# Differential attention: the second map's factor in a stage of its own, and another order of the last head's token tiles

## The chip, the cores and the metric

The kernel runs on one core of one Trainium2 chip. The metric is the time of one execution on the device, in microseconds (us), the median of several runs. A core has engines that run side by side and wait for each other by semaphores: PE (TensorE, matrix products and transposes), DVE (VectorE), ACT (ScalarE), POOL (GpSimd) and SP, which issues the transfers. Each engine works through its own queue strictly in order: an instruction that waits holds everything behind it on its engine.

## The reference, cut to what matters

The reference is a chain of two model blocks. The change lies in one part, the differential attention of the second block's second layer (`diff_attention`), 8 heads, 528 tokens (16 meta tokens and 512 others):

```python
def attn_map(qb, kk):
    lg = jnp.einsum('bqhd,bshd->bhqs', qb, kk).astype(jnp.float32) * scale + bias
    return jax.nn.softmax(jnp.where(mask, lg, NEG_INF), axis=-1)

a = attn_map(q1b, k1) - lam * attn_map(q2b, k2)
return jnp.einsum('bhqs,bshd->bqhd', a.astype(vb.dtype), vb)
...
o = rms_norm(o, sub_g) * (1.0 - lam_init)
return o.reshape(B, Tp, N_HEADS * B_V_DIM) @ w_o
```

So each head has two softmax maps; the second, times `lam`, is subtracted from the first, and the difference is applied to the values. Since each head's output is normalized afterwards, a common factor of a row may be left in it until then.

## The kernel before, in words

`layer_b` computes this layer. A unit is one head `h` and one tile `b` of 128 query tokens, `b` from 1 to 4; unit `b` sees `L` = 16 + 128 b keys (144, 272, 400 or 528), so `b` = 4 is the longest. The 32 units go through a software pipeline, `pipeline`: in round i, each letter of `STAGES_B` runs one stage on the unit that entered `lag` rounds ago, in the order of the letters.

- `l` and `m` (lag 0): the logits of the first and the second map on PE (tile `lg`).
- `s` and `r` (lag 0): `soft` for either map. DVE adds the bias and finds the row's extreme (L1633, and L1637 where two halves are needed), ACT takes the exponential and, as it goes, the row sum (tile `p`, L257). The first map's sum goes to a column of `sn` (`G["e"]`), the second's to a column of `sxb` (`s`).
- `d` (`s_diff`, lag 2): the factor of the second map, -lam times the first sum over the second, by a reciprocal on DVE (L1908) and two small ACT instructions on `sxb`; then `p` = `p2` times factor plus `p` on DVE, a scalar_tensor_tensor. I call this last one the combine.
- `t` (`turn`, lag 4): PE transposes `p` into `tp`, ACT copies it to `pt`.
- `o` (`s_out`, lag 6): PE multiplies with the values (`po`), DVE copies the result into `o`, ACT squares it.

After a head's last unit, `ends` puts three steps into `late`, one per round: the scaling of `o` (DVE and ACT on `sn`), the transposes `ot` with ACT's `ah`, and DVE's `al`. Only then can the head's share of the output projection run.

Between the stages `more` hands out filler for PE, by the credits of `FILL_B`: first the projections that make the later heads' queries, keys and values (tiles `hq` and `tg`; DVE scales them by `rb` into `hd`, ACT squares `hd` into `hsq`, PE sums `hsq` into `hs`, from which ACT makes the norm `hf`), and, when these are used up, the first part of the output projection (`wo`). The small products of the meta tokens (`ml`, `mo`) are handed out likewise. Weights come by transfer into `ws`, and ACT and POOL split them into a high part `wh` and a low part `wl`; POOL also makes the low parts `kx` and `qx` of keys and queries. Tiles in PSUM (`hq`, `tg`, `lg`, `tp`, `po`, `hs`, `wo` and the like) share eight banks in turn, so a product may wait until an earlier tile in its bank has been read.

The order of all instructions is as written, so PE's queue is set when the program is built.

Of the kernel before, what the change touches and what calls it, by code (L numbers as in the profile page):

```python
# [48 lines left out]
SQ_A, SQ_B = 0, 0  # L49
LN_EXP = "natural_log_exp_and_others"  # L50
TOP_V, TOP_D, TOP_R, TOP_E = (1, 1, 1, 1, 2), 275, 270, 60
STAGES_A, STAGES_B = "ldmtosw", "tlsdmro"
FILL_A, FILL_B = {"t": 1, "l": 1, "o": 2, "w": 2}, {"t": 0.868, "l": 1.017, "m": 1.562, "o": 1.471, "r": 0.7, "d": 0.1, "s": 0.1}
META_A, OUT_A, EARLY_B = 9, 2, 3
SUMS, ENDS = 3, 7
# [2 lines left out]
ORDER_B = (2, 3, 1, 4)  # L58
# [171 lines left out]
class K:  # L230
# [9 lines left out]
    def t(self, dt=F32, name="t", n=TB):  # L240
        x = self.pool.tile([128, TB], dt, name=name, tag="t")
        return x[:, :n] if n != TB else x
# [13 lines left out]
    def act(self, out, x, f=AF.Identity, **k):  # L256
        self.nc.scalar.activation(out, x, f, **k)  # L257
# [4 lines left out]
    def stt(self, out, in0, scalar, in1, op0, op1, **k):  # L262
        self.nc.vector.scalar_tensor_tensor(out, in0, scalar, in1, op0=op0, op1=op1, **k)  # L263
# [1050 lines left out]
    def head_sums(self, sq, ones, dim):  # L1314

        f = self.t(F32, "hf")
        for c in self.HALVES:
            S_ = self.sm("hs")[:, 0:264]
            for y in sq:
                self.mm(S_, ones[y.dtype], y[:, c], y is sq[0], y is sq[-1])  # L1320
            self.act(f[:, c], S_, AF.Ln, bias=self.eps[1e-6], scale=1.0 / dim)
        self.act(f, f, AF.Exp, scale=-0.5)
# [97 lines left out]
    def layer_a(self, hs, norm, hg):  # L1420
# [175 lines left out]
        def end(i):  # L1596
            if i == len(U) + OUT_A:
                self.out_late("w_oa", ao, out, 2, range(KD))

        a, b, c = LAG_A  # L1600
        S_ = {"m": (s_mask, 0), "t": (self.turn, 2 + b), "d": (s_share, 2 + a), "l": (s_logits, 2),
              "o": (s_out, 2 + c), "s": (s_soft, 2), "w": (s_low, 2 + c)}
        self.pipeline(U, S_, STAGES_A, more, lambda i: i >= META_A and meta and meta.pop(0)(), end)
        assert not meta and not topk
# [135 lines left out]
    def layer_b(self, hs, norm, hx):  # L1740

        nc, A, v, t, stt, dve, act = self.nc, self.A, self.v, self.t, self.stt, self.dve, self.act
# [49 lines left out]
        def place(h):  # L1792
            if ao[h] is None:
                ao[h] = t(F32R, "ah"), t(F32R, "al")
            return ao[h]
# [16 lines left out]
        def turn_o(o, n, w=4):  # L1812
            tp = self.sm("ot")
            for j in range(w):
                nc.tensor.transpose(tp[:, n * j:n * j + n], o[:n, 128 * j:128 * j + 128], self.ident[:n, :n])
            return tp[:, :w * n]

        def low(lo, ps, hi):
            stt(lo, ps, sub, hi.bitcast(F32), MUL, SUB)

        def ends(G):

            def turn():
                G["tp"] = turn_o(G["o"], 128)
                act(place(G["h"])[0][:, META:T], G["tp"], scale=sub)

            def last():
                hi, lo = (x[:, META:T] for x in ao[G["h"]])
                low(lo, G["tp"], hi)
                ready[1].add(G["h"])  # L1830

            return [lambda: scale(G["o"], G["e"], 128), turn, last]
# [43 lines left out]
            next(steps)  # L1876
        U = []
        for h in range(8):
            G = {"h": h}
            U += [{"b": b, "h": h, "G": G} for b in ORDER_B]  # L1880

        def s_logits(u, i):
            h = u["h"]
            q0, L = self.queries(u["b"])
            while ("q", h) not in done:
                next(steps, None)
            u["ps", i] = self.pair_logits(i, done["q", h], slice(q0, q0 + 128), done["k", h], L)

        def s_soft(u, i):
            h, b, G = u["h"], u["b"], u["G"]  # L1890
            L = self.queries(b)[1]
            if "e" not in G:
                G["e"] = stat()
                for k in ([0, 1] if h == 0 else [h + 1] if h < 7 else []):
                    self.bias[k] = self.load_bias(self.bias_d[k])
                if h:
                    self.bias[h - 1] = None
            if i == 0:
                u["s"] = self.small.tile([128, 8], F32, name="sxb", tag="sxb", bufs=8)
            s = u["s"]  # L1900
            x = u["p", i] = t(F32, "p", L)
            self.soft(x, u.pop(("ps", i)), self.bias[h][:, T - L:], s[:, 2 * i:2 * i + 2], s[:, 6 + i:7 + i],
                      s[:, 4:5] if i else G["e"][:, 3 + b:4 + b])

        def s_diff(u):

            s, b = u["s"], u["b"]
            nc.vector.reciprocal(s[:, 4:5], s[:, 4:5])  # L1908
            act(s[:, 4:5], s[:, 4:5], scale=nlam)
            act(s[:, 5:6], s[:, 4:5], scale=u["G"]["e"][:, 3 + b:4 + b])  # L1910
            u["p"], p2 = u.pop(("p", 0)), u.pop(("p", 1))
            stt(u["p"], p2, s[:, 5:6], u["p"], MUL, ADD)

        def s_out(u):
            G, b = u["G"], u["b"]
            if "o" not in G:
                G["o"] = t(F32, "o", 512)
            while ("v", u["h"] // 2) not in done:
                next(steps)
            o = self.pv(u, vh, tokens=True)  # L1920
            nc.vector.tensor_copy(G["o"][:, 128 * b - 128:128 * b], o)
            junk = self.b2.tile([128, 128], mybir.dt.bfloat16, name="oj", tag="oj", bufs=2)
            act(junk, o, AF.Square, accum_out=G["e"][:, b - 1:b])
            if b == ORDER_B[-1]:
                late.extend(ends(G))

        restored = []
# [58 lines left out]
            return late or others  # L1986

        a, b, c = LAG_B
        S_ = {"t": (self.turn, b), "d": (s_diff, a), "o": (s_out, c)}
        for i in range(2):  # L1990
            S_["lm"[i]] = (lambda u, i=i: s_logits(u, i)), 0
            S_["sr"[i]] = (lambda u, i=i: s_soft(u, i)), 0
# [58 lines left out]
```

## Time and profile before

| what | us |
|---|---|
| median of 3 runs | 2362.16 |
| lowest and highest of them | 2360.67, 2363.61 |
| the profiled execution | 2363.21 |
| its span in the trace | 2361.4 |
| the pipelined rounds of this attention in the trace, about | 1712 to 1960 |

The span is what the trace covers, from the first to the last instruction; the profiled execution's own time has 1.8 us more around it, and is itself 1.05 us above the median of the runs. A time in the trace is counted from the span's start. "Busy" is time in which an engine works on an instruction. "PEclk" is the TensorE clock that was granted, as a share of full speed.

### The profile page before, as it was taken

What the parts mean: (1) busy time and instruction counts of PE and PEld (TensorE: products, weight loads), DVE (VectorE), ACT (ScalarE), POOL (GpSimd) and SP (SyncE); (2) the same over time, 40 slices, a digit from 0 to 9 for tenths busy, and PEclk for the clock granted to TensorE, in tenths of its full rate; (3) what the DMA queues carried; (4) which work ended last, traced back from release to release, by engine and by line L of the source; (5) the groups of instructions that cost most, each with busy time, mean ns of one, the idle gap of its engine ahead of it and who ended that gap; (6) DMA issues with size and microseconds to landing.
All of it is one profiled execution on the core that took longest, in us unless ns stands there. A gap on an engine that the chain in (4) does not pass through costs nothing.

```text
span 2361.4 us, 36818 instructions
## 1 busy us (share of the span) xinstructions
PE 2286.5 (97%) x14560; PEld 2052.0 (87%) x14560; DVE 1296.8 (55%) x2492; ACT 982.4 (42%) x1814; POOL 1066.4 (45%) x608
## 2 busy tenths in 40 slices
PE   7999999999999999998999999999999989999999
PEld 5777787878888888888889999999998888989898
DVE  7767995566573022129974734435456656625443
ACT  3445543352243133344454423324466654424332
POOL 0434534456434434665533443434764443444433
PEclk9999999999999999999999999999999999999999
DMA  8324434525443223342102332323322122332322
GB/s 281 108 90 130 145 104 138 171 85 169 129 161 107 90 89 91 91 135 91 55 10 85 93 110 72 108 72 90 95 73 73 50 64 63 90 107 81 109 79 90
DMA packets 95980, 240.68 MB, mean 102 GB/s; under 512 B 10560, under 2 KB 26048, under 8 KB 95808
## 3 DMA queue, kind: packets, MB, share of 16 engines
q1 hardware_dynamic: 95808, 238.32, 33.0%
q8 instruction: 115, 1.88, 0.3%
q14 instruction: 57, 0.47, 0.1%
HBM read 230.72 MB, written 4.33 MB: 100 GB/s over the span
## 4 chain that ended last, share of the span: by engine, by line
PE 73%; DVE 14%; ACT 7%; issue 3%; DMA 2%; POOL 1%; SPq 0%; ACTq 0%; DVEq 0%; POOLq 0%
PE mm L260 54%; PE dn L260 9%; PE hq L260 2%; DVE cv L263 2%; PE tg L260 2%; ACT wh L210 1%; DVE xbc L263 1%; PE po L260 1%; ACT p L257 1%; PE lg L260 1%; DVE score L1476 1%; DMA ada<-in_w_ada_dram 1%; DVE p L263 1%; DVE pw L245 1%; DVE hd L245 1%
## 5 line engine op out<-in xcount | busy, mean ns | idle before, releaser
L266 POOL TENSOR_TENSOR wl<-ws,wh 128x1024 fp32r<-128x1024 f32 (+3 forms) x353 | 836.3, 2374 | 1084.8 <-ACT wh L210 1002.2
L260 PE MATMUL mm<-hh,wh 128*128 128x264 f32 (+3 forms) x2280 | 610.9, 322 | 10.5 <-ACT hh L257 7.6
L260 PE MATMUL mm<-hh,wl 128*128 128x264 f32 (+3 forms) x2280 | 605.6, 320 | 1.5 <-POOL wl L266 1.5
L260 PE MATMUL mm<-hl,wh 128*128 128x264 f32 (+3 forms) x2280 | 605.7, 320 | 1.4 <-DVE hl L263 0.7
L210 ACT CAST wh<-ws 128x1024 fp32r<-128x1024 f32 (+3 forms) x361 | 365.2, 1020 | 218.7 <-PE dn L260 83.7
L260 PEld LDWEIGHTS mm<-hh,wh 128*128 128x128 f32 x2280 | 381.7, 190 | 47.8 <-ACT hh L257 9.6
L260 PEld LDWEIGHTS mm<-hl,wh 128*128 128x128 f32 x2280 | 380.5, 189 | 38.9 <-DVE hl L263 5.3
L260 PEld LDWEIGHTS mm<-hh,wl 128*128 128x128 f32 x2280 | 381.3, 190 | 33.1 <-POOL wl L266 2.3
L263 DVE SCALAR_TENSOR_TENSOR cv<-u,vecs,cv 128x527 f32<-128x527 f32 (+3 forms) x176 | 185.9, 1056 | 87.6 <-ACT cv L257 84.5
L260 PE MATMUL dn<-ch,wl 128*128 128x264 f32 (+1 forms) x528 | 140.7, 321 | 0.0
L260 PE MATMUL dn<-ch,wh 128*128 128x264 f32 (+1 forms) x528 | 140.7, 321 | 0.0
L260 PE MATMUL dn<-cl,wh 128*128 128x264 f32 (+1 forms) x528 | 140.6, 320 | 0.0
L245 DVE TENSOR_TENSOR u<-mm,rb 128x264 f32<-128x264 f32 (+1 forms) x176 | 67.3, 424 | 108.2 <-PE mm L260 107.4
L257 ACT ACTIVATE cv<-u,vecs 128x528 f32<-128x528 f32 (+1 forms) x88 | 72.5, 824 | 115.2 <-DVE u L245 114.9
L260 PE MATMUL hq<-hh,wh 128*128 128x264 f32 x384 | 116.6, 304 | 1.6 <-ACT pt L1668 0.9
L260 PE MATMUL hq<-hh,wl 128*128 128x264 f32 x384 | 109.8, 286 | 2.7 <-POOL wl L266 2.7
L260 PE MATMUL hq<-hl,wh 128*128 128x264 f32 x384 | 110.1, 287 | 0.0
L263 DVE SCALAR_TENSOR_TENSOR junk<-ada,cs 128x512 bf16<-128x512 f32 x96 | 101.6, 1096 | 12.2 <-DMA ada<-in_w_ada_dram 12.0
L260 PE MATMUL mm<-ul,wh 128*128 128x512 f32 x256 | 100.9, 394 | 0.0
L260 PE MATMUL mm<-uh,wl 128*128 128x512 f32 x256 | 100.8, 394 | 0.0
L260 PE MATMUL mm<-uh,wh 128*128 128x512 f32 x256 | 100.7, 394 | 0.0
L260 PEld LDWEIGHTS dn<-ch,wl 128*128 128x128 f32 x528 | 87.6, 188 | 7.8 <-POOL wl L266 0.3
(368 smaller groups left out, 4177.3 us busy)
## 6 DMA issues: line engine op xcount, KB each, us to landing
ws<-in_w_up_dram SPq DMA_DIRECT2D x120, 512.0 KB, 3.6
ws<-in_w_in_dram SPq DMA_DIRECT2D x65, 512.0 KB, 3.6
ada<-in_w_ada_dram SPq DMA_DIRECT2D x96, 256.0 KB, 5.6
ws<-in_w_down_dram SPq DMA_DIRECT2D x32, 512.0 KB, 3.7
ws<-in_w_dn_dram SPq DMA_DIRECT2D x32, 512.0 KB, 3.5
E<-acs_d SPq DMA_DIRECT2D x32, 256.0 KB, 4.4
ws<-in_w_bs_dram SPq DMA_DIRECT2D x16, 512.0 KB, 3.7
ws<-in_w_ia_dram SPq DMA_DIRECT2D x15, 512.0 KB, 3.6
```

The source lines that it names most:

```text
L210: k.nc.scalar.copy(hi[:, :n_], st[:, :n_])
L245: self.nc.vector.tensor_tensor(out, in0, in1, op=op)
L257: self.nc.scalar.activation(out, x, f, **k)
L260: self.nc.tensor.matmul(out, a, b, start=start, stop=stop)
L263: self.nc.vector.scalar_tensor_tensor(out, in0, scalar, in1, op0=op0, op1=op1, **k)
L266: (eng or self.nc.vector).tensor_tensor(out, x, hi.bitcast(F32), op=SUB)
L1476: nc.vector.match_replace(s, m8, s, GONE)
```

## The change

`s_diff` is split in two. The reciprocal and the two small ACT instructions become the stage `f` (`s_factor`, lag 1), which stands behind `r` in each round; `s_diff` (lag 2) keeps only the combine. And the last head takes its tiles in the order 4, 3, 2, 1 where before it took 2, 3, 1, 4, as all other heads still do. `f` has no entry in `FILL_B`, so it hands out no filler, and no instruction is added or taken away.

```diff
-STAGES_A, STAGES_B = "ldmtosw", "tlsdmro"
+STAGES_A, STAGES_B = "ldmtosw", "tlsdmrfo"
...
-            G = {"h": h}
-            U += [{"b": b, "h": h, "G": G} for b in ORDER_B]
+            G = {"h": h, "order": ORDER_B if h < 7 else (4, 3, 2, 1)}
+            U += [{"b": b, "h": h, "G": G} for b in G["order"]]
...
-        def s_diff(u):
+        def s_factor(u):
 
             s, b = u["s"], u["b"]
             nc.vector.reciprocal(s[:, 4:5], s[:, 4:5])
             act(s[:, 4:5], s[:, 4:5], scale=nlam)
             act(s[:, 5:6], s[:, 4:5], scale=u["G"]["e"][:, 3 + b:4 + b])
+
+        def s_diff(u):
+
+            s = u["s"]
             u["p"], p2 = u.pop(("p", 0)), u.pop(("p", 1))
             stt(u["p"], p2, s[:, 5:6], u["p"], MUL, ADD)
...
-            if b == ORDER_B[-1]:
+            if b == G["order"][-1]:
                 late.extend(ends(G))
...
-        S_ = {"t": (self.turn, b), "d": (s_diff, a), "o": (s_out, c)}
+        S_ = {"t": (self.turn, b), "f": (s_factor, 1), "d": (s_diff, a), "o": (s_out, c)}
```

On DVE, in the round whose two softmaxes have `L` = 400, near 1827 us of the trace, these rows stand before:

```order
L1633 ISA p,sxb<-lg,bias 128x400
L1633 ISA sxb 128x1
L1908 RECIPROCAL sxb<-sxb 128x1
L263 SCALAR_TENSOR_TENSOR p<-p,sxb 128x528
L245 TENSOR_TENSOR hd<-hq,rb 128x264
L1633 ISA p,sxb<-lg,bias 128x400
L1633 ISA sxb 128x1
L1921 COPY o<-po 128x128
```

and these with the change:

```order
L1633 ISA p,sxb<-lg,bias 128x400
L1633 ISA sxb 128x1
L263 SCALAR_TENSOR_TENSOR p<-p,sxb 128x528
L245 TENSOR_TENSOR hd<-hq,rb 128x264
L1633 ISA p,sxb<-lg,bias 128x400
L1633 ISA sxb 128x1
L1909 RECIPROCAL sxb<-sxb 128x1
L1926 COPY o<-po 128x128
```

The combine (128x528 here) keeps its place; the reciprocal, now of the unit one round younger, stands behind the second softmax.

On ACT the same round reads so, with what goes and what comes (`kx` and `hsq` belong to a later head's projection, `p,sn` is the exponential of the first map, `p,sxb` that of the second):

```order
 L1390 CAST kx<-hd 64x528 x2
 L257 ACTIVATE p,sn<-p,sxb 128x400
-L257 ACTIVATE sxb<-sxb,lam 128x1
-L257 ACTIVATE sxb<-sxb,sn 128x1
 L257 ACTIVATE hsq<-hd 128x528
 L210 CAST wh<-ws 128x1024
 L257 ACTIVATE p,sxb<-p,sxb 128x400
+L257 ACTIVATE sxb<-sxb,lam 128x1
+L257 ACTIVATE sxb<-sxb,sn 128x1
 L257 ACTIVATE oj,sn<-po 128x128
```

The two small instructions leave the place behind the first exponential and come behind the second.

At the end of the rounds, when no unit enters any more, DVE's queue changes like this (`mo` is the meta tokens' output, `o` and `sn` belong to head 6 and its scaling):

```order
-L1908 RECIPROCAL sxb<-sxb 128x1
-L263 SCALAR_TENSOR_TENSOR p<-p,sxb 128x144
-L1921 COPY o<-po 128x128
+L263 SCALAR_TENSOR_TENSOR p<-p,sxb 128x272
+L1909 RECIPROCAL sxb<-sxb 128x1
+L1926 COPY o<-po 128x128
 L245 TENSOR_TENSOR sn<-sn 16x2
 L263 SCALAR_TENSOR_TENSOR sn<-sn 16x2
 L245 TENSOR_TENSOR mo<-mo,sn 16x256
-L1908 RECIPROCAL sxb<-sxb 128x1
-L263 SCALAR_TENSOR_TENSOR p<-p,sxb 128x528
```

The last unit's combine follows behind the last of these rows: with the change it is 128x144 instead of 128x528, and no reciprocal stands right ahead of it.

## Rows read from the trace of the kernel before

**Rows 1.** The page's first part: PE's busy time, share, instructions.

```profile
PE 2286.5 (97%) x14560; PEld 2052.0 (87%) x14560; DVE 1296.8 (55%) x2492; ACT 982.4 (42%) x1814; POOL 1066.4 (45%) x608
```

**Rows 2.** Busy time by stretch: length, each engine, granted clock, DMA.

```profile
core 0: us, PE busy (x) PEld busy (x) DVE busy (x) ACT busy (x) POOL busy (x), PEclk, DMA share, GB/s
1712.00:1945.00 233.00, 217.27 (x1700) 208.60 (x1699) 139.80 (x425) 149.32 (x455) 118.68 (x82) 0.97 0.22 65
1945.00:1960.00 15.00, 9.81 (x78) 8.98 (x76) 7.25 (x21) 7.35 (x25) 0.07 (x1) 1.00 0.04 15
1724.00:1730.00 6.00, 5.83 (x32) 5.52 (x33) 1.70 (x8) 5.05 (x10) 2.14 (x2) 0.72 0.01 3
1840.00:1846.00 6.00, 5.34 (x36) 5.30 (x37) 2.34 (x13) 5.57 (x14) 4.76 (x4) 0.72 0.48 132
1908.00:1916.00 8.00, 7.19 (x40) 6.87 (x41) 3.89 (x16) 5.16 (x16) 5.17 (x4) 0.57 0.33 94
```

**Rows 3.** What PE waited for, 1712 to 1945: us, times, longest.

```profile
PE hs L260 <- ACT hsq L257: 7.2, 6, 1.9
PE ml L260 <- POOL qk L1785: 2.6, 2, 2.2
PE po L260 <- DVE mp L245: 1.5, 1, 1.5
PE wo L260 <- POOL wl L266: 1.2, 1, 1.2
PE hq L260 <- ACT pt L1668: 0.9, 1, 0.9
PE wo L260 <- DVE sn L1843: 0.9, 1, 0.9
PE lg L260 <- DMA qx<-qz: 0.8, 1, 0.8
PE ot L1815 <- DVE o L245: 0.3, 1, 0.3
PE ot L1815 <- DVE sxb L1908: 0.3, 1, 0.3
```

**Rows 4.** What DVE waited for, the same stretch, the longest in total.

```profile
DVE p L263 <- ACT sxb L257: 51.7, 32, 3.6
```

**Rows 5.** Instructions on the tile sxb: count, ns shortest/median/longest, first, last.

```profile
L1908 DVE RECIPROCAL sxb<-sxb x32: 141/153/160, 1719.6 to 1944.0; 128x1 f32<-128x1 f32 x32
L257 ACT ACTIVATE sxb<-sxb,lam x32: 277/278/296, 1721.3 to 1944.2; 128x1 f32<-128x1 f32 x32
L257 ACT ACTIVATE sxb<-sxb,sn x32: 294/295/296, 1721.6 to 1944.5; 128x1 f32<-128x1 f32 x32
L263 DVE SCALAR_TENSOR_TENSOR p<-p,sxb x32: 367/921/3357, 1721.9 to 1944.8; 128x272 f32<-128x272 f32 x8, 128x400 f32<-128x400 f32 x8, 128x144 f32<-128x144 f32 x8, 128x528 f32<-128x528 f32 x8
```

**Rows 6.** Order of time near 1830 us: start, duration, instruction [idle before].

```profile
1827.44 2.70 POOL L266 TENSOR_TENSOR kx<-hd,kx 64x528 fp32r<-64x528 f32 x2 [0.54 <-POOL qk L1785]
...
1829.25 1.46 DVE L263 SCALAR_TENSOR_TENSOR p<-p,sxb 128x528 f32<-128x528 f32 x1 [2.05 <-ACT sxb L257]
1830.63 0.42 DVE L245 TENSOR_TENSOR hd<-hq,rb 128x264 f32<-128x264 f32 x1
...
1831.08 0.64 ACT L257 ACTIVATE hsq<-hd 128x528 f32<-128x528 f32 x1 [1.86 <-DVE hd L245]
...
1831.78 1.16 PE L260 MATMUL hs<-hsq,halves 128*128 128x264 f32 x4 [1.90 <-ACT hsq L257]
```

**Rows 7.** Order of time in the last rounds, the same columns.

```profile
1944.84 0.77 DVE L263 SCALAR_TENSOR_TENSOR p<-p,sxb 128x528 f32<-128x528 f32 x1 [0.69 <-ACT sxb L257]
1945.53 0.28 DVE L1921 COPY o<-po 128x128 f32<-128x128 f32 x1
...
1947.66 0.66 PE L1815 MATMUL ot<-ident,o 128*128 128x128 f32 x4 [2.14 <-DVE o L245]
...
1948.70 2.73 PE L260 MATMUL po<-v,pt 128*128 128x128 f32 x22
...
1953.67 0.66 PE L1815 MATMUL ot<-ident,o 128*128 128x128 f32 x4 [2.24 <-DVE o L245]
```

## The prediction

> **What bounds the kernel now.** I read the page's first part, then busy time by stretch, then the waits of PE, of DVE and of ACT in the stretch that the change touches, and last the order of time at single places. PE is busy for 97% of the span [rows 1], so only the time in which PE stands still, or runs at a lower clock, can be won. By stretch [rows 2]: from 1712 to 1945 us, the rounds of the attention, PE is busy for 217.3 of 233 us, so 15.7 us are idle; in the last rounds, 1945 to 1960, it is busy for 9.8 of 15, so 5.2 are. ACT is busy for 64% and DVE for 60% of the rounds: neither has too much work, so PE's idle time comes from order, from what stands ahead of what in a queue. The nine rows of PE's waits add up to the same 15.7 us [rows 3]. Most of it, 7.2 in six waits, is for `hsq`, the squares from which the later heads' norms are summed. A third loss is the clock: in three short stretches the granted clock is 0.72, 0.72 and 0.57 of full [rows 2], so PE falls between its two levels, 1.2 and 2.4 GHz. That costs about 6 x 0.28 = 1.7, 1.7 and 8 x 0.43 = 3.4 us, 6.8 in all. The first follows the `hs` wait that ended at 1724, the second the `ml` wait, the third the waits for `wl` and `qx`. All I can win or lose here is then 15.7 + 5.2 + 6.8 = 27.7 us, about 1.2%.
>
> **Where the idle time comes from.** DVE waits 51.7 us, 32 times, for the two small ACT instructions on `sxb` [rows 4]: 1.6 us for each unit. Before the change the combine needs a reciprocal made just ahead of it and, behind that, two small instructions of ACT, which stand behind the first map's exponential in ACT's queue. Near 1830 us this is seen whole [rows 6]: the combine starts after 2.05 us of waiting; behind it stands `hd`, at 1830.63; ACT was idle for 1.86 us for that `hd` and squares it at 1831.08; PE was idle for 1.90 us and starts `hs` at 1831.78. The same chain, a stalled combine and behind it `hd`, stands ahead of the other five `hs` waits.
>
> **What the change moves.** The reciprocal (0.15 us) and the two ACT instructions (0.28 and 0.30) run 32 times as before [rows 5], 23 us of work, none added. They come behind the second softmax of the round before, so that a combine finds its factor ready when the round's first softmax is done. No transfer and no instruction of POOL or SP changes its place, and PE's queue differs only in the last head. The terms:
>
> 1. *The `hs` waits.* They are 1.2 us on average, and the stall of the combine ahead of them is 1.6. With the stall gone `hd` comes early enough in all six, if the combine then runs. It reads two tiles from SBUF, and it is long where POOL works: near 1830 it took 1.46 us for 528 columns and ended 0.57 us after POOL's `kx` had (1827.44 + 2.70 = 1830.14), while the last one took 0.77 [rows 6, 7]. In the order of time, POOL works in three of the six places at the time to which the combine moves. I take 5.5 of 7.2; bounds 0 and 7.2.
> 2. *Other waits behind the combine on DVE:* `ml` 2.6 (its `qk` comes from an `hd` two combines later), `hq` 0.9 (a bank freed by `pt`, behind the second exponential), `wo` 0.9, `ot` 0.3 and 0.3, together 5.0 [rows 3]. I take 3.5; bounds 0 and 5.0.
> 3. *Waits that POOL sets:* `po` behind `mp` 1.5 (DVE's scaling of `o`, under POOL), `wl` 1.2, `qx` 0.8, together 3.5 [rows 3]. The combine is not their last cause. I take 0.5; bounds 0 and 3.5.
> 4. *The clock.* The stretches at 1724 and 1840 follow waits that go by terms 1 and 2; I count their 3.4 us back and leave the third. Bounds 0 and 6.8.
> 5. *The last rounds.* `ot` of head 6 waits 2.14 us for `o` [rows 7]. Its last copy, at 1945.53, stands right behind the last combine, which waited 0.69 us and took 0.77. With the change the factor is there, and the combine has 144 columns; the shortest of all took 0.37 [rows 5]. So 0.69 + 0.40 = 1.1 us. Behind this `ot` there were 5 transposes and 22 passes of `po` in 2.73 us; with tile 1 last there are 2 and 18, which saves 4 x 0.124 = 0.5 us and, at the same price, 0.4 for the transposes. The longer products of tile 4 now lie ahead of `ot`, inside its wait. The end of head 7 (2.24 us of waiting for its scaling) is as long as before. Together 2.0; bounds 0 and 2.9.
> 6. *Waits that come up instead.* When PE arrives some 9 us earlier, what POOL makes for it (term 3, of which 3.0 remain) comes into sight more often. I put this at 2.0, two thirds of it; bounds 0 and 4.
>
> Sum: -5.5 - 3.5 - 0.5 - 3.4 - 2.0 + 2.0 = -12.9 us. The profiled execution took 2363.2, so 2350.3; it was 1.05 above the median of the runs, so 2349.3 against that median.
>
> What hides the moved work: ACT's second exponential runs while DVE makes the reciprocal, and the factor then has until the next round's first softmax. If that cover is gone, because DVE reaches the reciprocal late (some filler of DVE stands ahead of it, at the place shown none), then ACT stands before the two small instructions, and behind them `oj` and `pt` are late, and so `tp`'s bank and PE's next product. The lag of two rounds from `turn` to the output covers `pt` itself, not the bank. The new order in the last head puts 528 columns into two rounds in a row and then less in each; PE showed no wait in the rounds of that head up to the `wo` wait of 0.9, so I cost this at nothing.
>
> **The rivals.**
>
> *The combine stalls at POOL instead.* POOL is busy for 118.7 of 233 us [rows 2], 51%, in instructions of 1.4 us. A combine that starts earlier meets one in half the cases and ends behind it. Then about half of terms 1 and 2 and one of the two clock stretches stay: -3.5 - 2.0 - 1.7 - 2.0 + 2.0 = -7.2, 2355. For it: combines took from 0.37 to 3.36 us with a median of 0.92 [rows 5]. Against it: the stalls under POOL are in the trace of before already, and the wait for ACT is paid on top of them; only where the wait covered POOL's time is it replaced. The Trainium skill ("SBUF — State Buffer", section on the two separate sides) says that GpSimd and a VectorE instruction with two SBUF inputs take a shared port pair as an exclusive lock, held for the whole instruction, and that the loser blocks fully. The trace agrees near 1830 (the combine ended 0.57 us after `kx`). By that rule taken alone the wait would only change its name at the places where POOL works; that is the 2355 worked out above.
>
> *It is hidden.* ACT, not DVE, may be what is late: its queue has casts of weights and keys and two exponentials in each round, and `hsq` may be held by these once `hd` is early. Then about 1 us of the `hs` waits and the 2 us of the last rounds are won: 2359. Against it: ACT was idle for 1.86 us ahead of `hsq` [rows 6], and it is free for 36% of the rounds.
>
> *It is slower.* The reciprocal stands behind the second softmax and behind a filler's instruction on DVE in many rounds. If these hold it for longer than the second exponential takes, ACT stands still with `pt` behind it, and PE waits for the bank as in the `hq` row, 0.9 us [rows 3]. Once per head in eight heads is +7 us with nothing won, 2369. It decides where the hold is over about 0.6 us in most rounds. Against it: DVE's own waits leave it idle for 40% of the time, and the reciprocal itself takes 0.15 us.
>
> **How the numbers follow.** I give the forecast 0.55 (its own range 2343 to 2355), the stall at POOL 0.20, the hidden case 0.15 and the slower one 0.10. A measurement of this kernel can tell about 0.2%, 4.7 us, from no change. Faster by more, under 2357.4, is the forecast and four fifths of the first rival: 0.71. Within is the rest of it and most of the hidden case: 0.19. Slower is 0.10. With every term at its best bound and nothing new it would be about 2337, which I hold unlikely; the range leaves out the slower case and a little at both ends: 2343 to 2361.
>
> **What the profile after would show.** DVE's wait of the combine for `sxb` falls from 51.7 us to under 10. PE's waits for `hsq` fall from 7.2 to under 2, that of `ml` from 2.6 to under 1. PE's idle time in the rounds falls from 15.7 to 6 to 9, and the granted clock is full near what was 1724 and 1840. The `ot` of head 6 waits about 1 us instead of 2.14, and the last rounds are 2 us shorter. If the combines have grown longer by as much as their waits fell, the stall at POOL holds; if the `hsq` waits stay while ACT is no longer idle ahead of them, the hidden case; if ACT waits for the reciprocal and PE for `pt`, the slower one. I would be wrong altogether if the clock fell in other places instead: each fall costs as much as one of the larger terms.

## The result, and the profile after

| kernel | median, us | lowest and highest | runs |
|---|---|---|---|
| before, beside it | 2362.89 | 2360.67, 2363.86 | 4 |
| changed | 2344.88 | 2343.96, 2346.55 | 4 |

The ratio is 0.9926, with a 95% interval of 0.9909 to 0.9943: the change saves 0.74%, 17.5 us, and 18.0 between the two medians. The profiled execution of the changed kernel took 2343.96 us, 19.25 less than that of before, and its span is 2342.0 us. The prediction was 2349.3, with a range of 2343 to 2361.

The page's first part of the changed kernel answers to [rows 1] (busy us, share, instructions of each engine):

```profile
PE 2278.8 (97%) x14560; PEld 2047.2 (87%) x14560; DVE 1308.0 (56%) x2492; ACT 981.0 (42%) x1814; POOL 1069.2 (46%) x608
```

PE does the same 14560 instructions in 7.7 us less of busy time; how much of that is the clock, the windows tell. In busy time by stretch, with the columns of [rows 2] (the mean granted clock is the first number behind the counts), the rounds now end near 1936 and not near 1954:

```profile
1712.00:1930.00 218.00, 212.51 (x1713) 206.48 (x1712) 148.82 (x432) 150.47 (x463) 121.49 (x82) 0.98 0.24 70
1930.00:1945.00 15.00, 12.07 (x87) 11.37 (x86) 7.38 (x16) 6.81 (x19) 2.40 (x1) 0.89 0.00 1
```

From 1712 to 1930 PE is idle for 5.5 of 218 us and in the last rounds for 2.9; before, it was 15.7 and 5.2. The waits of PE in the changed kernel, from 1712 to 1950 (us in total, times, longest), answer to [rows 3]:

```profile
PE wo L260 <- POOL wl L266: 3.2, 1, 3.2
PE ot L1815 <- DVE o L245: 2.6, 2, 2.2
PE po L260 <- DVE mp L245: 1.2, 1, 1.2
PE wo L260 <- ACT ah L257: 0.4, 1, 0.4
PE lg L260 <- ACT oj L257: 0.3, 1, 0.3
PE wo L260 <- DVE al L263: 0.3, 1, 0.3
PE hs L260 <- ACT hsq L257: 0.2, 1, 0.2
```

Of the 7.2 us for `hsq`, 0.2 are left; `ml`, `hq` and `qx` have no row at all. The one wait that has grown is `wl`, from 1.2 to 3.2. DVE's waits in the same stretch have no row for the combine any more, where [rows 4] had 51.7 us; the longest is now one for PE:

```profile
DVE o L1926 <- PE po L260: 13.4, 14, 2.7
```

So the order of dependence has turned round: DVE waits for PE, and not PE, by way of `hd` and ACT, for DVE. The same is seen at the place of [rows 6], in the order of time of the changed kernel (start, duration, instruction, in brackets the idle time before it and what ended it):

```profile
1816.42 0.76 DVE L263 SCALAR_TENSOR_TENSOR p<-p,sxb 128x528 f32<-128x528 f32 x1
1817.15 2.70 POOL L266 TENSOR_TENSOR kx<-hd,kx 64x528 fp32r<-64x528 f32 x2 [0.88 <-ACT kx L1390]
1817.64 0.43 DVE L245 TENSOR_TENSOR hd<-hq,rb 128x264 f32<-128x264 f32 x1 [0.46 <-PE hq L260]
1818.33 0.63 ACT L257 ACTIVATE hsq<-hd 128x528 f32<-128x528 f32 x1
1821.67 1.05 PE L260 MATMUL hs<-hsq,halves 128*128 128x264 f32 x4
```

The combine starts without a wait and takes 0.76 us; it ends at 1817.18, just as `kx` starts on POOL at 1817.15; before the change it began 1.81 us behind `kx`, and took 1.46. `hd` then waits for PE's own `hq`, and `hsq` is finished at 1818.96, 2.7 us before PE asks for it. The combines on tile `sxb` of the changed kernel (ns shortest/median/longest; [rows 5]):

```profile
L263 DVE SCALAR_TENSOR_TENSOR p<-p,sxb x32: 350/846/2583, 1719.7 to 1927.3; 128x272 f32<-128x272 f32 x8, 128x400 f32<-128x400 f32 x8, 128x144 f32<-128x144 f32 x8, 128x528 f32<-128x528 f32 x8
```

Grouped by shape, the 32 combines take 9.8 + 9.6 + 9.2 + 6.5 = 35.1 us in the changed kernel and 11.6 + 8.5 + 7.1 + 6.5 = 33.7 before: they gave up 51.7 us of waiting and took back 1.4. By the single durations, 17 of the 32 lasted more than 1.2 times the shortest of their shape before, and 16 do with the change. The last rounds, in the order of time ([rows 7]):

```profile
1927.31 0.35 DVE L263 SCALAR_TENSOR_TENSOR p<-p,sxb 128x144 f32<-128x144 f32 x1
1927.59 0.27 DVE L1926 COPY o<-po 128x128 f32<-128x128 f32 x1
1929.71 0.66 PE L1815 MATMUL ot<-ident,o 128*128 128x128 f32 x4 [0.39 <-DVE o L245]
1930.42 2.17 PE L260 MATMUL po<-v,pt 128*128 128x128 f32 x18
1934.84 0.66 PE L1815 MATMUL ot<-ident,o 128*128 128x128 f32 x4 [2.24 <-DVE o L245]
```

The `ot` of head 6 waits 0.39 us instead of 2.14, 18 passes follow instead of 22 (the other four now stand ahead of it, the 224 of all heads are the same), and the end of head 7 waits 2.24 us as before. One more view sorts the saving by place. `ot` is the transposed output of a head; its first and last matmul mark points that every version passes. The row on tile `ot` of before, and then that of the changed kernel (the two times are the first and the last start):

```profile
L1815 PE MATMUL ot<-ident,o x32: 270/272/332, 1777.9 to 1954.1; 128*128 128x128 f32 x32
```

```profile
L1815 PE MATMUL ot<-ident,o x32: 270/272/331, 1773.3 to 1935.2; 128*128 128x128 f32 x32
```

Up to the first `ot`, which lies 65 us inside the rounds, 4.6 us are saved; between the first and the last `ot` 176.2 - 161.9 = 14.3; behind the last one, to the span's end, 407.3 - 406.8 = 0.5. Nothing comes from earlier parts of the kernel: the first logits of the rounds start at the same time in both profiles, first before and then with the change:

```profile
L260 PE MATMUL lg<-kx,qz x80: 228/287/543, 1706.2 to 1933.4; 128*128 128x264 f32 x32, 128*128 128x272 f32 x16, 128*128 128x400 f32 x16, 128*128 128x144 f32 x16
```

```profile
L260 PE MATMUL lg<-kx,qz x80: 227/287/538, 1706.2 to 1917.8; 128*128 128x264 f32 x32, 128*128 128x272 f32 x16, 128*128 128x400 f32 x16, 128*128 128x144 f32 x16
```

### The profile page after: what moved, and what is told of

It is laid out like the page before. It is cut to its first block, busy times and chain, and to the rows that moved or that the text cites. A ratio compares the mean times of both kernels' runs of the same rounds, so it can differ in the third digit from the quotient of the medians.

```text
span 2342.0 us, 36824 instructions
## 1 busy us (share of the span) xinstructions
PE 2278.8 (97%) x14560; PEld 2047.2 (87%) x14560; DVE 1308.0 (56%) x2492; ACT 981.0 (42%) x1814; POOL 1069.2 (46%) x608
## 4 chain that ended last, share of the span: by engine, by line
PE 78%; DVE 12%; ACT 4%; issue 3%; DMA 1%; POOL 1%; SPq 0%; ACTq 0%; DVEq 0%; POOLq 0%
PE mm L260 54%; PE dn L260 10%; PE hq L260 4%; PE tg L260 2%; DVE cv L263 2%; PE po L260 1%; PE lg L260 1%; ACT wh L210 1%; DVE xbc L263 1%; PE wo L260 1%; DVE score L1476 1%; DVE pw L245 1%; PE hs L260 1%; DMA ws<-in_w_in_dram 1%; PE yd L260 1%
## 5 line engine op out<-in xcount | busy, mean ns | idle before, releaser
L263 DVE SCALAR_TENSOR_TENSOR junk<-ada,cs 128x512 bf16<-128x512 f32 x96 | 107.4, 1156 | 16.8 <-DMA ada<-in_w_ada_dram 16.8
```

## The experiments

My theory: the wait of the combine for a factor that went through ACT held `hd` up, and with it PE; any way of having the factor ready early gives the gain. The rivals were those of the prediction: ACT's queue, a stall at POOL, and a gain that is really the last head's order. The experiments were timed in three groups, each kernel in 4 to 11 runs beside 15 of the kernel before, which had medians of 2360.5 (first group: the first four experiments below), 2362.8 (second: the next four) and 2361.9 us (third). A kernel is compared with the kernel before of its own group.

The traces give two more numbers for each. One is the interval between first and last `ot`. The other is what the clock cost from 1712 to 2100, summed over slices of 2 us, each counted as 2 x (1 - granted clock).

| kernel | median, us | ratio, 95% interval | `ot` to `ot`, us | clock, us |
|---|---|---|---|---|
| before | | 1 | 176.2 | 8.5 |
| changed | 2344.9 | 0.9926 (0.9909 to 0.9943) | 161.9 | 5.1 |
| factor alone | 2347.5 | 0.9945 (0.9932 to 0.9957) | 163.8 | 5.1 |
| order alone | 2360.1 | 0.9996 (0.9987 to 1.0005) | 173.4 | 5.1 |
| factor on DVE, ACT's work kept | 2350.4 | 0.9956 (0.9943 to 0.9968) | 166.3 | 5.1 |
| detour longer by two instructions | 2372.0 | 1.0050 (1.0037 to 1.0062) | 182.1 | 8.6 |
| changed, once more | 2343.5 | 0.9921 (0.9908 to 0.9935) | 161.9 | 5.1 |
| changed, restores spread | 2342.5 | 0.9916 (0.9902 to 0.9929) | 159.7 | 3.4 |
| changed, factor by one DVE instruction | 2344.2 | 0.9925 (0.9912 to 0.9939) | 160.1 | 1.7 |
| changed, low parts on DVE | 2363.0 | 1.0002 (0.9994 to 1.0011) | 170.3 | 6.9 |
| detour longer by one instruction | 2367.5 | 1.0023 (1.0014 to 1.0032) | 180.1 | 8.5 |
| changed, both additions | 2342.6 | 0.9915 (0.9901 to 0.9928) | 159.4 | 3.4 |
| changed, factor at the round's start | 2354.5 | 0.9964 (0.9951 to 0.9976) | 165.7 | 3.4 |

**The two halves.** The first kernel has the new stage and the old order:

```diff
-            G = {"h": h, "order": ORDER_B if h < 7 else (4, 3, 2, 1)}
+            G = {"h": h, "order": ORDER_B}
```

> The factor's stage alone, with the last head's tiles in the old order. Theory (the combine's wait for ACT, on DVE, held up what PE needs): nearly all of the 17 to 18 us that the whole change brought, less the part of the last rounds that goes by the order (about 1 us of products and transposes and 0.4 of the shorter combine), so 15 to 17 us faster than before; PE's waits for hsq under 1 us in all. Rival A (the gain is the order of the last head and what it does to the last rounds): under 5 us. Rival B (a good part is only the clock, which falls or not by chance): between 8 and 12 us with the hsq waits gone all the same.

The second is the kernel before with the new order alone:

```diff
-            G = {"h": h}
-            U += [{"b": b, "h": h, "G": G} for b in ORDER_B]
+            G = {"h": h, "order": ORDER_B if h < 7 else (4, 3, 2, 1)}
+            U += [{"b": b, "h": h, "G": G} for b in G["order"]]
```

> The last head's tiles in the order 4, 3, 2, 1 alone, with the factor made where it was before. Theory: 1 to 2 us faster, from the shorter combine ahead of head 6's last copy (0.4 us) and from fewer products and transposes behind its ot (0.9 us); PE's waits for hsq unchanged at about 7 us. Rival A: 10 us or more. If the two effects don't add up to the whole change, they share something.

The factor alone took 13.0 us off, under the 15 to 17 expected, and its interval (10.2 to 16.1) reaches into the 8 to 12 of rival B. The trace decides against that rival: PE's waits from 1700 to 1975, without the one for `sq` behind the rounds, add up to 20.8 us before and 9.9 here, so most of the 13.0 is waiting and not the clock. The order alone took 0.4 off, which its interval does not tell from nothing. PE's waits for `hsq`, first with the factor alone, then with the order alone:

```profile
PE hs L260 <- ACT hsq L257: 0.2, 1, 0.2
```

```profile
PE hs L260 <- ACT hsq L257: 8.0, 7, 1.9
```

Yet in the traces the order shortens the rounds both times, by 176.2 - 173.4 = 2.8 us without the early factor and by 163.8 - 161.9 = 1.9 with it. Head 6's `ot` wait falls by 0.9 both times (2.14 to 1.24, and 1.28 to 0.39), so the order is not seen to be worth more once the factor is early. In times, the whole change stands 0.0019 to 0.0024 of the ratio, 4 to 6 us, below the factor alone. The rounds hold 2 of these; for the rest there is no place in the trace, and as the intervals overlap it is not shown that there is a rest.

**The wait itself.** In the next kernel the program order is that of before, ACT still does its two small instructions, on columns of `sxb` that nothing reads, and the combine's factor comes from one DVE instruction right behind the reciprocal:

```diff
-                u["s"] = self.small.tile([128, 8], F32, name="sxb", tag="sxb", bufs=8)
+                u["s"] = self.small.tile([128, 10], F32, name="sxb", tag="sxb", bufs=8)
...
-            act(s[:, 4:5], s[:, 4:5], scale=nlam)
-            act(s[:, 5:6], s[:, 4:5], scale=u["G"]["e"][:, 3 + b:4 + b])
+            act(s[:, 8:9], s[:, 4:5], scale=nlam)
+            act(s[:, 9:10], s[:, 8:9], scale=u["G"]["e"][:, 3 + b:4 + b])
+            self.ts(s[:, 5:6], s[:, 4:5], nlam, u["G"]["e"][:, 3 + b:4 + b], MUL, MUL)
```

> The kernel before, but DVE makes the factor itself, by one instruction of its own behind the reciprocal, so the combine no longer waits for ACT; ACT's two small instructions stay where they were, into columns that nobody reads. Theory (DVE's wait is the stall): 13 to 17 us faster, as with the factor's stage, though ACT's queue is as full as before. Rival C (the gain comes from the two instructions leaving their place in ACT's queue ahead of hsq and the pt copies): no more than 3 us faster.

It took 10.1 us off, under the 13 to 17 expected and well over the 3 of rival C. PE's waits in its rounds, 1712 to 1950:

```profile
PE ot L1815 <- DVE o L245: 4.0, 2, 2.2
...
PE ml L260 <- POOL qk L1785: 1.5, 1, 1.5
...
PE hs L260 <- ACT hsq L257: 0.6, 2, 0.4
```

`hsq` falls from 7.2 to 0.6 us although ACT's load is unchanged and its small instructions stand where they stood. So it was the round trip to ACT, not the two instructions' load on ACT's queue. The next two go the other way and repeat the second small ACT instruction, twice more or once more for each unit, in the kernel before (the first has this line twice):

```diff
             act(s[:, 5:6], s[:, 4:5], scale=u["G"]["e"][:, 3 + b:4 + b])
+            act(s[:, 5:6], s[:, 4:5], scale=u["G"]["e"][:, 3 + b:4 + b])
```

> The kernel before with two more small ACT instructions, which write the factor again, ahead of each combine: the detour over ACT is 0.6 us longer per unit. Theory: DVE's wait for sxb rises by about 32 x 0.6 = 19 us, to 70, and since some 12 waits of PE hang behind it, PE loses 0.4 to 0.6 us in each: 4 to 8 us slower than before. Rival (the waits of PE are set by something else and the stall lies beside it): within 1 us of before.

> The kernel before, with the second small ACT instruction on sxb issued twice for each unit instead of once, half of the dose of the longer detour; the output is unchanged. The longer detour made DVE's wait for sxb 73.4 us instead of 51.7 and the time 11.5 us longer. If PE's time goes in proportion to that wait, half the dose gives a wait of about 62 us and a time 5 to 6 us longer than before. Rival: the time has a threshold, since hd is late by little at most places, and half a dose gives under 2 us.

They lost 11.5 and 5.6 us. The 73.4 us of the second expectation are 31 of the 32 waits, in a window that ends before the last; all of them make 74.8. DVE's wait for the combine, and PE's for `hsq`, first with two more instructions:

```profile
DVE p L263 <- ACT sxb L257: 74.8, 32, 4.2
```

```profile
PE hs L260 <- ACT hsq L257: 11.4, 7, 2.6
```

and DVE's wait with one more, where PE waited 9.3 us for `hsq`:

```profile
DVE p L263 <- ACT sxb L257: 64.4, 32, 3.9
```

With a DVE wait of 0 (the factor alone), 51.7, 64.4 and 74.8 us the time is 13.0 us under, at, 5.6 over and 11.5 over that of before. A microsecond of the wait is worth 13.0 / 51.7 = 0.25 us down to none (0.20 to 0.31 by the interval) and 11.5 / (74.8 - 51.7) = 0.50 us when it grows (0.38 to 0.63). The two pieces of the growth, 0.44 and 0.57, can't be told apart. My explanation, argued from this and not shown at each place: slack between `hd` and PE absorbs the early part of a wait, and the later part much less. The longer detour went past its expectation of 4 to 8 us. Two things in the traces bear on this. A longer wait is in part no loss to DVE: as it rose from 51.7 to 64.4 and 74.8, the combines behind it fell from 33.7 to 28.3 and 23.2 us, so DVE spends only 12.6 us more on wait and combine where the time grew by 11.5. And the detours give ACT 9.5 and 18.9 us more work, but ACT stood idle for `hd` ahead of six of the seven `hsq` for which PE waited with the longest detour, so there it was `hd` that was late, not ACT.

**Whether it must be a round ahead.** Here `f` stands at the start of the combine's own round, ahead of the transposes and the first softmax:

```diff
-STAGES_A, STAGES_B = "ldmtosw", "tlsdmrfo"
+STAGES_A, STAGES_B = "ldmtosw", "ftlsdmro"
...
-        S_ = {"t": (self.turn, b), "f": (s_factor, 1), "d": (s_diff, a), "o": (s_out, c)}
+        S_ = {"t": (self.turn, b), "f": (s_factor, a), "d": (s_diff, a), "o": (s_out, c)}
```

> The whole change with the factor's stage at the start of the combine's own round, ahead of the transposes and of the first softmax, instead of behind the second softmax of the round before. Between it and the combine lie one softmax of DVE and its exponential. Theory: the combine finds its factor ready all the same, DVE's wait for sxb is under 3 us in all, and the time is that of the whole change within 2 us. Rival: it is the full round ahead that counts, since ACT's two small instructions now stand ahead of the first exponential and behind the second of the round before: DVE waits 10 to 25 us for sxb, and 4 to 8 us of the gain are lost.

The ratio is 0.9964, so about half of the gain is gone, 9 to 10 us: the rival held in kind, though it gave 4 to 8 us and a DVE wait of 10 to 25. DVE's wait, ACT's wait, and the three longest of PE's waits in this kernel that the changed one does not have, or has far shorter:

```profile
DVE p L263 <- ACT sxb L257: 9.9, 11, 1.7
```

```profile
ACT sxb L257 <- DVE sxb L1909: 17.9, 13, 3.1
```

```profile
PE hq L260 <- DVE sxb L1633: 2.7, 1, 2.7
PE hs L260 <- ACT hsq L257: 1.7, 1, 1.7
PE hq L260 <- DVE mp L245: 1.4, 1, 1.4
```

DVE's wait is back only to 9.9 us. The new loss is on ACT: it stands 17.9 us in 13 waits, up to 3.1, for the reciprocal, which stands on DVE behind whatever came last in the round before (behind a scaling of `o` of 2.66 us at one of the two longest). In the changed kernel that row reads:

```profile
ACT sxb L257 <- DVE sxb L1909: 2.1, 4, 1.0
```

This is the first link of what the prediction called the slower case. The second link, PE waiting for `pt`, is only 0.5 us here, and how ACT's 17.9 us reach PE was not followed. Behind the second softmax the reciprocal is covered by the second exponential, and from the round's start it is not. The profiled run of this kernel was its fastest, 2350.3 against a median of 2354.5, so some 4 us of the loss are not in its trace.

**One DVE instruction.** The changed kernel, with the factor made by one DVE instruction in `f` and none of ACT:

```diff
-            act(s[:, 4:5], s[:, 4:5], scale=nlam)
-            act(s[:, 5:6], s[:, 4:5], scale=u["G"]["e"][:, 3 + b:4 + b])
+            self.ts(s[:, 5:6], s[:, 4:5], nlam, u["G"]["e"][:, 3 + b:4 + b], MUL, MUL)
```

> The whole change, with the factor in the same stage but made on DVE alone, one instruction in place of ACT's two. Theory (after the change the two instructions cost nothing where they stand, since no one waits for sxb): within 1.5 us of the whole change, for 18 us less work on ACT. Rival C (ACT's queue is what is late): 3 us or more faster than the whole change.

It changed the time by +0.7 us, which is nothing that can be told: once the factor is early, who makes it does not matter. The changed kernel itself was timed in the same group, as the measure of these additions.

> The whole change once more, beside the next three on one chip. If the factor's stage (0.9945) and the order (0.9996) act apart from each other, the ratio is about 0.994, 14 us; if the order is worth more once the factor is early, because head 6's last copy then waits for a short combine alone, it stays at 0.9925, 17 to 18 us.

It took 2343.5, a ratio of 0.9921 after 0.9926: the second of the two cases by its middle, but the interval of the first measurement (0.9909 to 0.9943) holds 0.994 too.

**The `wl` wait.** Where `steps` is used up, `restore` puts eight additions on POOL in one go, and `wl`, which PE needs next, stands behind them. The order of time in the changed kernel shows it, for POOL and for PE:

```profile
1880.04 11.13 POOL L248 TENSOR_TENSOR h<-hh,hl 128x528 f32<-128x528 f32 x8
1891.13 1.26 POOL L266 TENSOR_TENSOR wl<-ws,wh 128x512 fp32r<-128x512 f32 x1
1892.45 0.59 PE L260 MATMUL wo<-ah,wl 128*128 128x264 f32 x1 [3.20 <-POOL wl L266]
```

The next kernel hands out one addition for each step of the filler:

```diff
-                    if not restored:
-                        restored.append(restore())
+                    if len(restored) < KD:
+                        restored.append(restore(len(restored)))
...
-        def restore():
+        def restore(m):
 
-            for m, (hi, lo) in enumerate(hx):
-                hs[m] = t(F32, "h")
-                self.pol(hs[m], hi.bitcast(F32), lo.bitcast(F32), ADD)
+            hs[m] = t(F32, "h")
+            self.pol(hs[m], hx[m][0].bitcast(F32), hx[m][1].bitcast(F32), ADD)
```

> The whole change, with the eight POOL additions that restore h given out one per step of the early output projection, where they stand in one block of 11 us now. Theory (the wait of 3.2 us for wl is POOL's block, which PE now reaches sooner): that wait goes, and with it the fall of the clock right behind it, 3 to 5 us faster than the whole change. Rival (PE would wait at this place for another thing, qx or the weights' high part): within 1 us of the whole change.

It gained 1.0 us against the changed kernel, which is not clear of noise, and not 3 to 5. PE's waits in it, 1690 to 1975:

```profile
PE ot L1815 <- DVE o L245: 2.6, 2, 2.2
PE wo L260 <- POOL wl L266: 1.6, 1, 1.6
...
PE lg L260 <- DMA qx<-qz: 1.2, 1, 1.2
```

Five additions still come in a row, and `wl` waits 1.6 us. A wait for the copy of `qz` comes in, 1.2 us, and the clock falls elsewhere. The rounds are 2.2 us shorter by the trace, and no more than 1 us of that shows in the time.

> The whole change with the factor made by one DVE instruction instead of two of ACT, and the eight restores of h spread over POOL's queue. Alone, the first gave +0.7 us and the second -1.0 us against the whole change. Theory: nothing adds up beyond that, 2342 to 2344, a ratio to before of 0.991 to 0.9925. Rival: with both, ACT and POOL give PE room together, and the wl wait goes from 1.6 us to nothing: 2340 or under.

With both additions the ratio is 0.9915. That and the 0.9916 of the restores alone are the lowest of all, and neither interval excludes that of the changed kernel.

**POOL.** If POOL's work held the combines up, its low parts of `kx` and `qx` would be better on DVE:

```diff
-                return self.pair_queries(x, h % len(self.zq), nc.gpsimd)
-            return self.pair_keys(x, nc.gpsimd)
+                return self.pair_queries(x, h % len(self.zq))
+            return self.pair_keys(x)
```

> The whole change, with the low parts of the heads' keys and queries made by DVE, not POOL: POOL loses about 35 us of work in the rounds, DVE gets about 26 instructions of some 0.7 us, 18 us. If the combines are long because POOL works beside them, their mean falls from 1.10 us, towards the 0.56 that the shortest of each size come to. The time: the stall at POOL as a cause that PE feels would give 1 to 3 us back; if it lies beside PE's work, DVE's longer queue costs 0 to 4 us.

This was a miss on both sides: it lost 19.4 us, the whole gain. DVE has 18.0 us of `qx` and 11.1 of `kx` to do, by the groups of its rounds, and `hsq` is late again. PE's waits, and then one place in the order of time, first POOL's row, then DVE's:

```profile
PE hs L260 <- ACT hsq L257: 10.3, 6, 5.5
```

```profile
1894.86 11.78 POOL L248 TENSOR_TENSOR h<-hh,hl 128x528 f32<-128x528 f32 x8
...
1895.35 3.14 DVE L266 TENSOR_TENSOR kx<-hd,kx 64x528 fp32r<-64x528 f32 x2 [0.70 <-ACT kx L1390]
1898.51 1.18 DVE L245 TENSOR_TENSOR sn<-sn 128x4 f32<-128x4 f32 x1
1899.72 1.22 DVE L263 SCALAR_TENSOR_TENSOR sn<-sn 128x4 f32<-128x4 f32 x1
1901.51 1.23 DVE L245 TENSOR_TENSOR o<-o,sn 128x512 f32<-128x512 f32 x1 [0.57 <-ACT sn L257]
...
1902.89 1.30 DVE L263 SCALAR_TENSOR_TENSOR p<-p,sxb 128x272 f32<-128x272 f32 x1
1904.12 0.42 DVE L245 TENSOR_TENSOR hd<-hq,rb 128x264 f32<-128x264 f32 x1
```

`hd` comes behind six DVE instructions of about 1.2 us or more each, all of them inside POOL's eight additions, and PE waits 5.5 us at this one place. The combines did become shorter, 28.5 us in all (8.0 + 7.7 + 7.5 + 5.3), 6.6 under the changed kernel's, for 29.1 us of added work.

## Why the prediction was right, and where its sizes were off

The direction, the mechanism and the range held; the forecast was 4.4 us too high. Of the signs it named, PE's idle time in the rounds fell to 5.5 us where 6 to 9 stood, and the `ot` wait of head 6 to 0.39 where about 1 stood. By its own terms, from profile to profile:

1. *The `hs` waits:* 7.0 us of 7.2 are gone, where 5.5 were counted. The discount was for combines that stall at POOL. They grew by 1.4 us in all, and no `hd` behind them was late for PE by more than 0.2. One of the six, 0.59 us at 1819.91, had no combine ahead of its `hd`, as I had said of all, but four `al` that waited for ACT's `ah`; it went with the rest.
2. *Other waits behind the combine:* all 5.0 us are gone, where 3.5 were counted. It was the same discount.
3. *Waits that POOL sets:* `mp` went from 1.5 to 1.2 and `qx` from 0.8 to nothing, 1.1 where 0.5 was counted. `wl` grew, which belongs to term 6.
4. *The clock:* 3.4 us was counted. In this pair of profiles the cost from 1712 to 2100 fell from 8.5 to 5.1. Over the table it averages (8.5 + 5.1 + 8.6 + 8.5) / 4 = 7.7 us in the kernels in which the combine waits in full, and (5.1 + 5.1 + 5.1 + 5.1 + 3.4 + 1.7 + 3.4) / 7 = 4.1 in those in which it waits for almost nothing (without the two kernels that bring other waits). So the size fits. In the rounds the places were right too: the stretches at 1724 and 1840 are at full clock as promised, and the fall near 1894 stands behind the `wl` wait, as the third stretch did before, which the term left in place. Behind the rounds it was luck that nothing changed in sum: a fall of 1.7 near 1985 is gone and one near 1937 is new, and neither was counted. What I said would make me wrong altogether did happen at that one place.
5. *The last rounds:* 2.0 was counted. The `ot` of head 6 waits 2.14 - 0.39 = 1.75 us less. The prediction counted 0.9 of shorter products and transposes behind it besides 1.1 of waiting; but these products are not fewer, they moved ahead of `ot` into its wait, and so are part of the 1.75. By the traces of the order alone, 0.9 of it goes to the order.
6. *New waits:* 2.0 was counted. `wl` grew by 2.0, and `lg` 0.3 came in: 2.3. The waits for `ah` and `al` stood before as well, at 1955, behind the rows of [rows 3]. The place named was the right one, POOL.

With these sizes the sum is -7.0 - 5.0 - 1.1 - 3.4 - 1.8 + 2.3 = -16.0 us where it was -12.9. Its waits agree with PE's idle time, which fell from 15.7 + 5.2 to 5.5 + 2.9, by 12.5. The profiles differ by 19.25, so 3.3 are not assigned. They are not from before the rounds, since the first logits start at 1706.2 in both.

The step that was mis-sized is the discount on terms 1 and 2, 1.7 + 1.5 = 3.2 us, of which 3.0 were not needed. The argument for it (POOL is busy half the time, so half the combines run into it) is true of the combines, 16 of 32, but 17 of 32 were held up before as well: their stalls were already in the trace and nothing new to count. What PE sees is `hd`, and without 51.7 us of waiting DVE came to it early, at the place shown 2.7 us before PE asked for `hsq`, so that a combine may lose a microsecond. The 3.3 us that are not assigned are as large, so the discount is the largest error that could be placed and not the whole of it.

Of the rivals, the hidden case falls with the factor on DVE, in which ACT keeps its work and `hsq` is on time. The stall at POOL falls for this change, by the 1.4 us of its combines and by the 0.2 us that are left of `hsq`; with the low parts on DVE it does show, at one place. The slower case did not come up here, but its first link is real: from the round's start ACT waits 17.9 us for the reciprocal. Where the stage stands in its round matters, and not only that it comes before the combine.

## What to carry to other kernels

An instruction that waits at the head of an in-order queue costs what stands behind it, so look for what another engine needs from that queue and not for the waiting instruction itself. A small factor that goes over another engine and back should be made a stage earlier, or on the engine that uses it, and its own source must be covered where it now stands. The microseconds of a wait are not worth the same: here 0.25 us each down to none and 0.50 each when it grew, so one experiment that lengthens a wait says little of what shortening it will bring.

## What the runs showed of the hardware that was not expected

A DVE instruction with two inputs in SBUF can last as long as the POOL instruction beside it, even one of 4 columns. In the order of time of the changed kernel, near 1820 us and in the last rounds, the same scaling of 4 columns:

```profile
1820.02 2.37 POOL L266 TENSOR_TENSOR wl<-ws,wh 128x1024 fp32r<-128x1024 f32 x1 [0.17 <-POOL kx L266]
1820.40 2.01 DVE L245 TENSOR_TENSOR sn<-sn 128x4 f32<-128x4 f32 x1
...
1927.79 0.14 DVE L245 TENSOR_TENSOR sn<-sn 128x4 f32<-128x4 f32 x1
```

With POOL quiet it takes 0.14 us. Beside `wl` it takes 2.01 and ends at 1822.41, 0.02 us behind POOL's 1822.39. Of the 16 small instructions on `sn` with 4 columns in this kernel, the eight that began beside a POOL tensor_tensor ended 0.01 to 0.03 us behind one, and the other eight took 0.14 to 0.16 us. The instructions that read PSUM keep their length: 15 of the 26 `hd` and 13 of the 32 copies of `po` overlap an instruction of POOL, and all of them take 0.41 to 0.43 and 0.26 to 0.29 us. The Trainium skill ("SBUF — State Buffer", section on the two separate sides) describes an exclusive lock of a shared port pair, held for the whole instruction, with the loser blocked; these rows agree. In the changed kernel the price did not reach PE; with the low parts on DVE it did, at one place.

The granted clock fell at places that differ from run to run, also behind waits that are alike. Windows of the changed kernel, and then of the changed kernel with the factor by one DVE instruction, over the same `wl` wait of 3.2 us in both (the granted clock is the first number behind the counts):

```profile
1886.00:1902.00 16.00, 12.80 (x89) 12.23 (x87) 9.71 (x30) 6.65 (x19) 11.66 (x10) 0.79 0.17 55
```

```profile
1886.00:1902.00 16.00, 11.48 (x100) 10.91 (x99) 9.79 (x29) 8.45 (x21) 13.46 (x12) 1.00 0.17 51
```

The first lost 16 x 0.21 = 3.4 us to the clock, the second nothing. Over the thirteen profiles the clock's cost up to 600 us, which no edit touches, was between 1.7 and 8.6 us. A single profile is then good to some microseconds only, and a term for the clock can be tested by an average over kernels but not by one trace. What decides whether a given wait is followed by a fall stays open.
